# A decoder step's head: adaLN shift and scale in two halves of the features, a written order on every engine, and another product order for the first z pair

## The chip, the cores and the metric

The kernel runs on one core of one Trainium2 chip. The metric is the device time of one execution in microseconds (us), the median over runs.

## The reference

One layer of a hybrid decoder is computed for a prompt of 1024 tokens and for 8 samples of 8 tokens each (64 rows), in fp32, with a model width of 1024. What matters here is its beginning:

```python
mod = jax.nn.silu(c) @ w_ada + b_ada                  # c: 1 prompt row, 8 sample rows; w_ada 1024 x 3072
shift, scale, gate = jnp.split(mod, 3, axis=-1)
h = rmsnorm(x, norm_g) * (1 + scale[:, None]) + shift[:, None]
proj = h @ w_in                                        # w_in 1024 x 8224
u_pool, z_pool, z_ssm, xbc, dt_raw, g_raw = jnp.split(proj, SPLITS, axis=-1)
...                                                    # pooling branch, convolution, state-space scan
m = sigmoid(g_pool) * p + sigmoid(g_ssm) * s
x = x + gate[:, None] * (m @ w_o)                      # then a final rmsnorm
```

The outputs are y for prompt and samples and the new states of the pool, the convolution and the scan.

## The kernel before

All activations are held with the features on the 128 partitions and the 1088 tokens (1024 + 64) along the free axis, so h is eight tiles `k` = 0..7 of 128 x 1088. Every matmul operand is split into a rounded high half and the rest as a low half, and a product is three matmuls (high x high, high x low, low x high). Weights are split by `split` (L160): ScalarE copies the high half (L163) and GpSimd subtracts (L166).

**The head.** Tokens are cut into three blocks `BLK` of 256, 384 and 448 columns (2, 3 and 4 tiles of rows of x, the last one 64 rows). The steps are:

1. `x_load` (L195) of the first two row tiles on the SP queue, then `w_ada` for shift and scale: 16 loads (L226), per `k` one for shift and one for scale, 512 KB each. Weights of the first pair of outputs (`w_first`, L177) come between, then the other row tiles.
2. `x_norm(g3)` per block: ScalarE squares a row tile and sums it (L203), takes the root (L204), VectorE inverts and multiplies (L205, L206).
3. `x_turn` (L213): TensorE transposes the row tiles of one block for one `k` into PSUM.
4. The adaLN product (L247), 64 matmul steps into two PSUM banks `pm`; then both are copied (L259), transposed (L262) and brought into `md` (L264, L268): shift for tile `k` in `md[:, k]`, 1 + scale in `md[:, 8 + k]`.
5. `h_group(g3)` (L277): per `k`, scale and shift into `tf[k]`, the high half `hh_` on ScalarE (L311, or L299 for the first one), the low half `hl_` on VectorE or, for odd `k`, GpSimd (L283). For block 0 the source is `tf` itself (copied from PSUM at L236 or L238). For blocks 1 and 2 it is PSUM: even `k` on VectorE (L304), odd `k` on ScalarE (L302). The 64 sample columns of block 2 have a scale and shift of their own, two VectorE steps (L307, L309).
6. `first_unit` (L731): two output tiles of `g_ssm` over all eight `k`; per block and output tile 24 matmuls (L334 to L336), then ScalarE's sigmoid (L737) and a store.

**Behind it** stands a list of units: `late_loads` (L346), `dt_unit` (L631, three blocks, L638), `combine` (L446), then pairs of output tiles by Strassen's scheme. `combine` forms the sums S2, S3, S1 and S4 of quarters of h on VectorE (L465, L466, L467, L473), with high halves on ScalarE (L452) and low halves on VectorE or, for S4, on GpSimd (L453). A pair needs seven products, each of two half products of 12 matmuls with 272 columns (L534 to L536). Its weights are prepared by `pair_w` (L480): loads into `rawA`, sums on VectorE and one on GpSimd (L502), seven splits. The first pair is a z pair (`light[0]`), whose weight work carries a raised scheduling priority (`PRIO`); its products are taken in the order h11, S2, S3, S1, h12, h22, S4. Behind it comes `gate_unit(0)` (L818).

**What sets the order.** The instructions are put in order by the scheduler, from the program order, priorities and its own model of durations. In the head some instructions are bound behind others by `issue_after` with constants (`SQ`, `XT`, `TLAG`, `LAG`, `DIR`, `WK`, `PLO`). `in_line` (L1220) binds TensorE to program order in a later stage, the scan. PSUM has eight banks: three in `PA` and five in `PB`, the latter for transposes among others.

Of the kernel before, what the change touches and what calls it, by code (L numbers as in the profile page):

```python
# [14 lines left out]
PRI = 0  # L15
# [3 lines left out]
DIR = 1  # L19
LAG = 1  # L20

SQ = (1, 3, 5, 7, 7, 7, 7)
WK = 7

XT = {11: (0, 1), 12: (2, 3), 13: (4, 5), 15: (6, 7)}

PLO = (1, 3, 5, 7)
TLAG = 2
TCKW = dict(schedule_with_timeline_sim=True)

P = 128
# [25 lines left out]
def tile_pool_ssd_step(  # L57
# [140 lines left out]
    def x_norm(g3):  # L198
        for i in range((0, *XG)[g3], XG[g3]):
            xt, n = xr[i]  # L200
            sqj = pa.tile([P, D], F32, tag="rawA", name=nm("sqj"), bufs=3)
            with (tc.issue_after(h_ins[SQ[i - XG[0]]].ins) if g3 else ExitStack()):
                act(sqj[:n], xt[:n], AF.Square, accum_out=ss[:n, i:i + 1])  # L203
            act(rs[:n, i:i + 1], ss[:n, i:i + 1], AF.Sqrt, bias=eps[:n], scale=1.0 / D)  # L204
            V.reciprocal(rs[:n, i:i + 1], rs[:n, i:i + 1])  # L205
            V.tensor_scalar(xt[:n], xt[:n], rs[:n, i:i + 1], None, ALU.mult)  # L206

    def x_turn(g3, k):
        px = PB()
        c = 0  # L210
        for i in range((0, *XG)[g3], XG[g3]):
            xt, n = xr[i]
            nc.tensor.transpose(px[:, c:c + n], xt[:n, k * P:(k + 1) * P], ident[:n, :n])  # L213
            c += n
        return px

    for i in range(XG[0]):
        x_load(i)
    wraw = {}
    wbig = [Y4(hp, F32), Y4(hp, F32)]  # L220
    for k in range(KT):
        if k == WK:
            w_first = [wcols(C_G + D)(), prep(w_in[0, 0:512, C_G + D + P:C_G + D + 2 * P], 4)]
        for half in range(2):
            wraw[k, half] = wbig[k // 2][:, 2 * k % 4 + half, :D] if k < 4 else G((P, D))
            load(wraw[k, half], w_ada[0, k * P:(k + 1) * P, half * D:(half + 1) * D])  # L226
    x_norm(0)
    tf = [None] * KT

    def x0_turn(k, after=None):  # L230
        with (tc.issue_after(after.ins) if after is not None else ExitStack()):
            px = x_turn(0, k)
        w = BLK[0][1]
        tf[k] = tfp.tile([P, T], F32, tag="tf", name=nm("tf"), bufs=8)
        if k % 2:
            act(tf[k][:, :w], px[:, :w], AF.Copy)  # L236
        else:
            V.tensor_copy(tf[k][:, :w], px[:, :w])  # L238

    for k in range(KT):  # L240
        if all(k not in v for v in XT.values()):
            x0_turn(k)
    pm = [PB(), PB()]
    for k in range(KT):
        for half in range(2):
            for j in range(4):
                a_ins = mm(pm[half][32 * j:32 * j + 32, :256], scT[:, k, :], wraw[k, half][:, j * 256:j * 256 + 256],  # L247
                           start=(k == 0), stop=(k == KT - 1))
            for kx in XT.get(2 * k + half, ()):
                x0_turn(kx, a_ins)  # L250
    for i in range(XG[0], XG[1]):
        x_load(i)
    w_first[1] += prep(w_in[0, 512:1024, C_G + D + P:C_G + D + 2 * P], 4)
    for i in range(XG[1], XG[2]):
        x_load(i)
    md = const([P, 16, 9], "md")
    for half in range(2):
        mr = pa.tile([P, 256], F32, tag="rawA", name=nm("mr"), bufs=3)
        act(mr, pm[half][:, :256], AF.Copy)  # L259
        ps = PB()  # L260
        for i in range(2):
            nc.tensor.transpose(ps[:, i * P:(i + 1) * P], mr[:, i * P:(i + 1) * P], ident)  # L262
        m8 = slice(8 * half, 8 * half + 8)
        V.tensor_tensor(md[:, m8].rearrange("p (j i) b -> p j i b", i=2),  # L264
                        ps[:, :256].rearrange("p (i j b) -> p j i b", i=2, j=4)[:, :, :, 0:9],
# [8 lines left out]
    def hl_tile(k):  # L274
        return hb[1][:, k] if k < 4 else G((P, T), F32R)
# [1421 lines left out]
```

## Time and profile before

| what | value |
|---|---|
| median of 3 runs | 1329.92 us (1328.44 to 1330.29) |
| the profiled execution | 1329.25 us, its span 1327.5 us |
| granted TensorE clock, mean | 0.986 |
| TensorE busy | 1268.2 us, 96% |
| VectorE, ScalarE, GpSimd busy | 882.4, 697.3, 719.9 us |
| first product of the first pair of outputs | starts at 32.56 us |
| last product of the first z pair | starts at 111.69 us |

The profile gives start and duration of each instruction of one execution, what ended the idle time before it, and per stretch of time how long each engine was busy. PE is TensorE, PEld its weight loads, DVE VectorE, ACT ScalarE, POOL GpSimd, SP the engine whose queue issues most loads. In tables "L247" is a line of the kernel. Matmuls overlap, so durations of neighbouring ones are longer than the distance from start to start.

### The profile page before, as it was taken

Reading aid. Unit: us, or ns where it says so; the run is one execution under the profiler, and the core shown is the slowest. Engines: PE = TensorE matmul, PEld = TensorE weight load, DVE = VectorE, ACT = ScalarE, POOL = GpSimd, SP = SyncE. Lnnn points to the kernel's source line nnn. Section 1 sums busy time; section 2 is a strip of 40 time slices with the busy share of each in tenths; the row PEclk is TensorE's granted clock in tenths of the full one; section 3 lists DMA queues with packets and bytes.
Section 4 is the critical chain, followed back from the end, with each engine's and each line's share of the span. In section 5 each row is a group of like instructions: output and inputs, shape, how many; then the busy total and the mean of one; then the engine's idle time right before and its main releaser. Section 6 shows DMA issues by size and latency. Waiting matters only on the chain.

```text
span 1327.5 us, 26100 instructions
## 1 busy us (share of the span) xinstructions
PE 1268.2 (96%) x9575; PEld 1162.9 (88%) x9575; DVE 882.4 (66%) x1473; ACT 697.3 (53%) x1660; POOL 719.9 (54%) x589
## 2 busy tenths in 40 slices
PE   5889999999999999988999999999999999999998
PEld 2768999999999999978889989978987888998786
DVE  2794489778867856856566666378575777567433
ACT  3854436656656555635654464657887767301211
POOL 1357568868877876843444353456576656314000
PEclk9799999999999999989999999999999999999999
DMA  9338345635644564442557455999988665475621
GB/s 369 112 104 270 111 132 172 227 115 177 203 151 147 160 203 134 146 140 86 159 161 205 146 156 166 352 311 364 317 279 273 200 207 161 163 260 165 214 101 62
DMA packets 230521, 251.67 MB, mean 190 GB/s; under 512 B 31101, under 2 KB 173573, under 8 KB 230386
## 3 DMA queue, kind: packets, MB, share of 16 engines
q1 hardware_dynamic: 158260, 171.56, 40.7%
q10 hardware_dynamic: 72134, 78.45, 17.3%
q8 instruction: 76, 1.25, 0.4%
q14 instruction: 51, 0.42, 0.1%
HBM read 167.06 MB, written 83.01 MB: 188 GB/s over the span
## 4 chain that ended last, share of the span: by engine, by line
PE 75%; issue 7%; DVE 6%; DMA 6%; POOL 3%; ACT 3%; SPq 1%; ACTq 0%; DVEq 0%; POOLq 0%
PE ps L534 8%; PE ps L535 8%; PE ps L536 8%; PE mm L534 8%; PE mm L536 7%; PE mm L535 7%; PE mm L334 4%; PE mm L335 4%; PE mm L336 4%; PE ps L961 2%; PE ps L1645 2%; PE ps L1644 2%; PE ps L1643 2%; PE ps L1177 2%; PE ps L964 1%
## 5 line engine op out<-in xcount | busy, mean ns | idle before, releaser
L166 POOL TENSOR_TENSOR wlo<-rawA,whi 128x512 fp32r<-128x512 f32 x124 | 195.6, 1583 | 116.5 <-ACT whi L163 105.5
L166 POOL TENSOR_TENSOR wlo<-raw,whi 128x512 fp32r<-128x512 f32 x97 | 162.8, 1686 | 156.0 <-ACT whi L163 147.3
L334 PE MATMUL mm<-Y,whi 128*128 128x352 f32 (+3 forms) x504 | 172.8, 345 | 4.1 <-ACT Y L299 2.1
L335 PE MATMUL mm<-Y,whi 128*128 128x352 f32 (+3 forms) x504 | 167.0, 331 | 3.4 <-DVE Y L283 2.3
L336 PE MATMUL mm<-Y,wlo 128*128 128x352 f32 (+3 forms) x504 | 166.2, 330 | 0.0
L534 PE MATMUL mm<-Y,whi 128*128 128x272 f32 x496 | 146.3, 295 | 2.7 <-ACT dts L641 2.6
L536 PE MATMUL mm<-Y,wlo 128*128 128x272 f32 x496 | 143.4, 290 | 3.2 <-POOL wlo L166 3.2
L535 PE MATMUL ps<-Y,whi 128*128 128x272 f32 x496 | 144.1, 291 | 2.3 <-DVE Y L453 2.3
L534 PE MATMUL ps<-Y,whi 128*128 128x272 f32 x496 | 145.7, 294 | 0.0
L536 PE MATMUL ps<-Y,wlo 128*128 128x272 f32 x496 | 143.2, 289 | 0.0
L163 ACT ACTIVATE whi<-rawA 128x512 fp32r<-128x512 f32 x124 | 77.9, 628 | 123.9 <-PE ps L535 81.6
L535 PE MATMUL mm<-Y,whi 128*128 128x272 f32 x496 | 142.9, 288 | 0.0
L776 DVE SCALAR_TENSOR_TENSOR GA<-GA,cvT,GA 128x1112 f32<-128x1112 f32 x72 | 127.2, 1771 | 0.6 <-ACT GA L773 0.5
L163 ACT ACTIVATE whi<-raw 128x512 fp32r<-128x512 f32 x97 | 59.3, 627 | 94.0 <-DVE raw L502 42.3
L334 PEld LDWEIGHTS mm<-Y,whi 128*128 128x128 f32 x504 | 95.9, 191 | 11.7 <-issue 4.7
L335 PEld LDWEIGHTS mm<-Y,whi 128*128 128x128 f32 x504 | 96.4, 191 | 4.7 <-DVE Y L283 2.5
L534 PEld LDWEIGHTS mm<-Y,whi 128*128 128x128 f32 x496 | 93.4, 188 | 7.7 <-ACT dts L641 2.8
L536 PEld LDWEIGHTS mm<-Y,wlo 128*128 128x128 f32 x496 | 93.3, 188 | 4.5 <-POOL wlo L166 4.3
L534 PEld LDWEIGHTS ps<-Y,whi 128*128 128x128 f32 x496 | 94.0, 189 | 3.2 <-issue 2.9
L535 PEld LDWEIGHTS ps<-Y,whi 128*128 128x128 f32 x496 | 94.0, 190 | 3.1 <-DVE Y L453 2.7
L336 PEld LDWEIGHTS mm<-Y,wlo 128*128 128x128 f32 x504 | 96.1, 191 | 0.2
L536 PEld LDWEIGHTS ps<-Y,wlo 128*128 128x128 f32 x496 | 94.1, 190 | 0.0
(413 smaller groups left out, 3761.4 us busy)
## 6 DMA issues: line engine op xcount, KB each, us to landing
rawA<-in_w_in SPq DMA_DIRECT2D x46, 512.0 KB
dec<-acs_d SPq DMA_DIRECT2D x32, 512.0 KB
xbc<-GA ACTq DMA_DIRECT2D x24, 512.0 KB
xb<-xbc SPq DMA_DIRECT2D x32, 384.0 KB
rawA<-in_w_in SPq DMA_DIRECT2D x32, 256.0 KB
pw<-in_w_ssm_out ACTq DMA_DIRECT2D x32, 256.0 KB
ws<-ph ACTq DMA_DIRECT2D x32, 256.0 KB
ws<-pw SPq DMA_DIRECT2D x32, 256.0 KB
```

Of the source, the lines that this page charges most:

```text
L163: ins = act(hi[:, :, :ncols], raw[:, :, :ncols], AF.Copy)
L166: nc.gpsimd.tensor_tensor(lo[:, :, :ncols], raw[:, :, :ncols], hi[:, :, :ncols].bitcast(F32), ALU.subtract)
L334: mm(ps[:, :n], a, rh[k][:, o:o + n], start=(k == 0), stop=False)
L335: mm(ps[:, :n], a, rl[k][:, o:o + n], start=False, stop=False)
L336: mm(ps[:, :n], b, rh[k][:, o:o + n], start=False, stop=(k == nk - 1))
L534: mm(p, hi, ah, start=(k == 0), stop=False)
L535: mm(p, hi, al, start=False, stop=False)
L536: mm(p, lo, ah, start=False, stop=(k == 3))
L776: V.scalar_tensor_tensor(d[:, :n], rp[:, k:k + n], cvT[:, 24 * k + mc:24 * k + mc + 1], d[:, :n], ALU.mult, ALU.add)
L961: mm(o[hh], xd[:S, 2 * q + hh, :], dec[:S, 2 * q + hh], start=True, stop=state is None)
L1177: mm(pu, bt, xw.rearrange("p h d -> p (h d)"), start=True, stop=True)
L1643: mm(ps[:, :cw], mhk, wo[k][0][:, s], start=(k == 0), stop=False)
```

## The change

Shift and scale are computed in two halves of the features: part 0 for `k` 0..3, part 1 for `k` 4..7. Each load of `w_ada` now holds the part's 512 columns of shift and of scale. Five row tiles of x are loaded and normed ahead. `x_turn` copies every transposed tile to `tf`, on ScalarE or VectorE by turns, and `h_make` scales from there on VectorE for all tiles (for blocks 0 and 1 ScalarE makes the high half straight from `tf` with scale and shift). The first pair of outputs is taken by halves of the features: with `k` 0..3 for four and later five of six accumulators, then with `k` 4..7. The whole head is one function, `first`, and `in_line` binds each of the five engines to its written order there. `late_loads` is cut in two. For the first z pair the products run in the order h11, h12, h22, S2, S3, S1, S4, with the weights prepared in that order. The constants of the old order are gone.

```diff
+    def x_turn(g3, k):                       # transposes as before, then
+        o = BLK[g3][0]
+        if (k + g3) % 2:
+            act(tf[k][:, o:o + c], px[:, :c], AF.Copy)
+        else:
+            V.tensor_copy(tf[k][:, o:o + c], px[:, :c])
+    def ada_load(part, k):
+        w = wbig[k // 4][:, k % 4, :D] if part == 0 else G((P, D))
+        wraw[part, k] = w.rearrange("p (s c) -> p s c", s=2)
+        load(wraw[part, k], w_ada[0, k * P:(k + 1) * P, 0:2 * D].rearrange("p (s h c) -> p s h c", s=2, h=2)[:, :, part])
+    def ada_mm(part, k):
+        if k == 0:
+            pm[part] = PB()
+        for j in range(4):
+            mm(pm[part][32 * j:32 * j + 32, :256], scT[:, k, :], wraw[part, k][:, j // 2, j % 2 * 256:j % 2 * 256 + 256],
+               start=(k == 0), stop=(k == KT - 1))
+    def ada_end(part):                       # copy, two transposes, then scale and shift of four tiles
...
+    def h_make(g3, k):
...
+        if e == w:
+            act(hi, t, AF.Identity, scale=sc[:, 0:1], bias=sh[:, 0:1])
+        V.tensor_scalar(t[:, :e], t[:, :e], sc[:, 0:1], sh[:, 0:1], ALU.mult, ALU.add)
+        if e < w:
+            ts_ = t[:, e:w].rearrange("p (b i) -> p b i", i=8)
+            V.tensor_tensor(ts_, ts_, sc[:, 1:9].unsqueeze(2).to_broadcast([P, NB, 8]), ALU.mult)
+            V.tensor_tensor(ts_, ts_, sh[:, 1:9].unsqueeze(2).to_broadcast([P, NB, 8]), ALU.add)
+            act(hi, t, AF.Copy)
+        (nc.gpsimd if k % 2 else V).tensor_tensor(hl_[k][:, o:o + w], t, hi.bitcast(F32), ALU.subtract)
+    def in_line(engines, begin=False):       # each instruction behind the one traced before it on its engine
...
     def late_loads():                        # loads, then
+        yield
...                                           # the transposes
     def pair_w(c0, c1, pri, early):
                 diff(t2, t3, b11, ALU.add)
+                if early:
+                    add(b21)
+                    diff(b21, t2, b21, eng=nc.gpsimd)
+                    add(b21)
                 add(t2)
                 add(t3)
                 yield
                 diff(b12, b12, b11)
                 add(b12)
-                add(b21)
-                diff(t2, t2, b21, eng=nc.gpsimd)
-                add(t2)
+                if not early: ...
                 add(b22)
     def strassen(w, d0, d1, early=False):
+        if early:
+            def fifth(s, p):
+                out(d0, HF, s1, u3, ALU.subtract)(s, u3[:, s])
+                out(d1, HF, s1, c2)(s, p)
+                add(u2, u2)(s, p)
+            product(w[0], a_part(0, 0), lambda s, p: act(s1[:, s], p, AF.Copy))
+            product(w[1], a_part(0, 1), out(d0, 0, s1, c2))
+            product(w[2], a_part(1, 1), lambda s, p: act(u3[:, s], p, AF.Copy))
+            product(w[3], s_part(S2), add(s1, u2))
+            product(w[4], s_part(S3), add(u2, s1))
+            product(w[5], s_part(S1), fifth)
+            product(w[6], s4_part, out(d1, 0, u2, u2))
+            return
+    def first():
+        in_line(every, True)                  # all five engines
...
+        for i in range(5): x_load(i)
+        for k in range(KT):
+            ada_load(0, k)
+            if k == KT - 2: w_load(0, 0)
+        w_load(1, 0)
+        for i in range(5, 9): x_load(i)
+        for k in range(6): ada_load(1, k)
+        w_load(0, 1)
+        x_norm(0); x_norm(1); ada_mm(0, 0); ada_mm(0, 1); x_turn(0, 0); x_turn(0, 1)
+        x_norm(2); ada_mm(0, 2); x_turn(0, 2); x_turn(0, 3); x_norm(3); ada_mm(0, 3); x_norm(4); ada_mm(0, 4)
+        x_turn(1, 0); x_turn(1, 1); ada_mm(0, 5); x_turn(1, 2); x_turn(1, 3); ada_mm(0, 6)
+        x_turn(0, 4); x_turn(0, 5); w_split(0, 0); ada_mm(0, 7); ada_end(0)
+        h_make(0, 0..1); w_split(1, 0); h_make(0, 2..3); w_load(1, 1); ada_load(1, 6..7); next(late)
+        products(0, 0, range(4)); x_norm(5); h_make(1, 0..1); products(0, 1, range(4)); ada_mm(1, 0)
+        h_make(1, 2..3); x_norm(6); products(1, 0, range(4)); ada_mm(1, 1..2); x_norm(7); x_norm(8)
+        x_turn(0, 6); x_turn(0, 7); products(1, 1, range(4)); ada_mm(1, 3)
+        for k in range(4): x_turn(2, k); h_make(2, k)
+        x_turn(1, 4); x_turn(1, 5); products(2, 0, range(4)); ada_mm(1, 4..5); x_turn(1, 6); x_turn(1, 7); w_split(0, 1)
+        x_turn(2, 4); x_turn(2, 5); ada_mm(1, 6); w_split(1, 1); x_turn(2, 6); x_turn(2, 7); ada_mm(1, 7); ada_end(1)
+        next(late, None)
+        for bi in range(3):
+            for k in range(4, 8): h_make(bi, k)
+            for t in range(2):
+                products(bi, t, range(4 if bi < 2 or t == 0 else 0, 8))
+                done(bi, t)                   # sigmoid and store
+        in_line(every)
-    h_group(0)
-    x_norm(1)
-    x_norm(2)
-    units = [(lambda: w_first, first_unit), plain(late_loads), (dt_w, dt_unit), plain(combine), plain(to_conv),
+    first()
+    units = [(dt_w, dt_unit), plain(combine), plain(to_conv),
```

In this extract the calls of `first` are put several to a line, and `0..1` stands for a short loop or two calls; the order is that of the code.

307 lines of the change are left out of this document (170 added, 137 removed).

## The prediction

> **What bounds it now.** I read the page first, then the head in stretches, then its rows in order of time.
>
> ```profile
> PE 1268.2 (96%) x9575; PEld 1162.9 (88%) x9575; DVE 882.4 (66%) x1473; ACT 697.3 (53%) x1660; POOL 719.9 (54%) x589
> PE   5889999999999999988999999999999999999998
> PEclk9799999999999999989999999999999999999999
> ```
>
> TensorE is full from the fourth slice on. The room is in the first three slices (100 us), and the change touches nothing behind them. The stretches of the head show why; columns are start:end, length, busy us of PE, PEld, DVE, ACT, POOL, then granted clock, DMA share and GB/s.
>
> ```profile
> 25.30:32.50 7.20, 3.53 (x36) 1.75 (x36) 2.90 (x6) 3.84 (x9) 3.29 (x3) 1.00 1.07 380
> 32.50:40.50 8.00, 5.60 (x26) 5.40 (x27) 7.36 (x16) 6.22 (x17) 3.21 (x5) 0.57 0.86 271
> 40.50:49.20 8.70, 5.52 (x38) 4.13 (x37) 5.20 (x11) 8.64 (x17) 0.60 (x1) 0.89 0.55 130
> 49.20:54.40 5.20, 5.15 (x26) 5.09 (x25) 3.85 (x8) 5.18 (x13) 2.31 (x2) 0.53 0.20 68
> 54.40:74.20 19.80, 19.80 (x130) 16.29 (x129) 18.09 (x35) 10.75 (x20) 10.10 (x8) 1.00 0.08 29
> 74.20:101.70 27.50, 22.64 (x181) 17.84 (x180) 26.39 (x32) 14.82 (x28) 15.39 (x11) 1.00 0.46 141
> 101.70:111.90 10.20, 9.60 (x76) 9.24 (x74) 3.45 (x9) 6.52 (x13) 9.38 (x8) 1.00 1.01 328
> ```
>
> Until 32.5 the DMA is full and TensorE waits for the adaLN weights. From 32.5 to 101.7 VectorE is the fullest, and it and GpSimd hold each other up:
>
> ```profile
> 75.04 1.55 POOL L166 TENSOR_TENSOR wlo<-rawA,whi 128x512 fp32r<-128x512 f32 x1 [0.82 <-ACT whi L163]
> 75.36 1.82 DVE L473 TENSOR_TENSOR tf<-tf,tf 128x544 f32<-128x544 f32 x1
> 77.10 0.71 DVE L465 TENSOR_TENSOR tf<-tf,tf 128x544 f32<-128x544 f32 x1
> ```
>
> The operation that takes 0.71 us alone took 1.82 us, ending 0.6 us after GpSimd's did. So the SBUF work of the two is one queue, "the pair's time" below. The marks of the head:
>
> ```profile
> 14.97 0.64 PE L247 MATMUL ps<-Y,scT 128*32 128x256 f32 x8 [0.64 <-DMA Y<-in_w_ada]
> 16.24 0.64 PE L247 MATMUL ps<-Y,scT 128*32 128x256 f32 x8 [0.63 <-DMA Y<-in_w_ada]
> 28.82 0.64 PE L247 MATMUL ps<-G,scT 128*32 128x256 f32 x8 [0.69 <-DMA G<-in_w_ada]
> 31.91 0.60 ACT L299 ACTIVATE Y<-tf,md 128x256 fp32r<-128x256 f32 x1 [0.69 <-DVE md L268]
> 72.67 1.54 POOL L283 TENSOR_TENSOR G<-tf,G 128x448 fp32r<-128x448 f32 x1 [0.83 <-ACT G L311]
> 94.60 7.05 POOL L453 TENSOR_TENSOR Y<-tf,Y 128x544 fp32r<-128x544 f32 x4 [7.87 <-ACT Y L452]
> 111.69 0.29 PE L536 MATMUL ps<-Y,wlo 128*128 128x272 f32 x1
> 111.91 1.92 PE L818 MATMUL ps<-GA,scT 128*32 128x512 f32 x16
> ```
>
> The first scaled tile of h starts at 31.9, the last low half of h ends at 74.2, the Strassen sums end at 101.7, the first z pair at 111.9. Behind that point the program is the same, so the forecast is where 111.9 goes.
>
> **The load.** A 512 KB piece takes 16.24 - 14.97 = 1.27 us. Ahead of the last piece that the first shift and scale need stood 2 x tiles, 15 pieces and up to three quarter-megabyte weight loads; now stand 5 x tiles, 7 pieces and one. That is 5 to 6 pieces, 6.4 to 7.6 us, earlier; rows of half the length cost between nothing and a seventh of 8 x 1.27 us (380 against 328 GB/s in the rows of 25.3 and 101.7, both at a full DMA share; the latter mixes many short rows). I take 0.5, near the lower end because half a row is still longer than most of those, so 6.5. The three further norms and the turns stand in front in written order; I give them 0.5. First scaled tile: 31.9 - 6 = 26.
>
> **First half of the features, written order.** What each tile costs (mean ns is the figure behind the bar):
>
> ```profile
> L203 ACT ACTIVATE sqj<-Y 128x1024 f32<-128x1024 f32 x6 | 6.2, 1041 | 0.0
> L213 PE MATMUL ps<-ident,Y 128*128 128x128 f32 x52 | 10.0, 316 | 3.2 <-ACT tf L302 1.8 <-DVE Y L206 0.9 <-DVE tf L304 0.3
> L304 DVE TENSOR_SCALAR tf<-ps,md 128x384 f32<-128x384 f32 x8 | 5.2, 674 | 2.1 <-PE ps L213 2.1
> 37.19 0.41 DVE L304 TENSOR_SCALAR tf<-tf,md 128x256 f32<-128x256 f32 x1
> L307 DVE TENSOR_TENSOR tf<-ps,md 128x64 f32<-128x64 f32 x8 | 1.6, 217 | 0.0
> L311 ACT ACTIVATE G<-tf 128x448 fp32r<-128x448 f32 x4 | 2.3, 571 | 3.1 <-DVE tf L309 3.1
> L283 DVE TENSOR_TENSOR Y<-tf,Y 128x448 fp32r<-128x448 f32 x2 | 1.2, 622 | 0.2 <-ACT Y L311 0.2
> L283 POOL TENSOR_TENSOR Y<-tf,Y 128x256 fp32r<-128x256 f32 x2 | 1.6, 810 | 1.3 <-ACT Y L311 1.3
> L283 POOL TENSOR_TENSOR G<-tf,G 128x448 fp32r<-128x448 f32 x2 | 2.8, 1380 | 2.9 <-ACT G L311 2.9
> L166 POOL TENSOR_TENSOR wlo<-raw,whi 128x512 fp32r<-128x512 f32 x9 | 12.3, 1373 | 35.3 <-ACT whi L163 35.3
> ```
>
> Before, blocks 1 and 2 were scaled straight out of PSUM (odd tiles at L302 on ScalarE, even ones at L304 on VectorE), which took nothing from GpSimd. Now they are copied out first and scaled from SBUF on VectorE: 16 scalings of 0.41 (the 256 form) to 0.67 us join the pair's time, some 8 us. A copy of 448 columns the trace does not show: between 0.4 and 0.7 us; I take 0.7, the nearest form from PSUM. Per stage:
> - Block 0, four tiles: pair's time 4 x 0.41 + 2 x 0.42 + 2 x 0.81 + one split 1.37 = 5.5, to 31.5.
> - A norm and block 1: 0.8 + 4 x 0.5 + 2 x 0.55 + 2 x 1.1 = 6.1 with waits for ScalarE under it, less overlap 1: to 36.6.
> - Three norms (ScalarE 3 x 1.04 and their roots) beside two groups of 12 products and the next loads' products: 5, to 41.6.
> - Block 2: an even tile is copy 0.7, scale 0.5, two sample steps 0.4, high half 0.57 on ScalarE, low half 0.62, one behind the other because VectorE stands in written order: 2.8. An odd one is 0.9 plus its wait for GpSimd's 1.4 of the tile before, less overlap: 1.7. Four tiles: 9, to 50.6.
> - The tail on TensorE: four adaLN steps of 0.64, 2.6, and 22 transposes, which at 10.0 / 52 us each are 4.2 if nothing lies beside them; they alternate with those steps and with the copies, and two accumulators of the products hold two of the five banks that they turn through, so I take half, 2.1: 4.7. Then the 3.1 us from the last adaLN product to the first scaled tile (28.82 to 31.91). Second half begins at 58. The second half's loads hide under this: 13 pieces more behind the first half's 22 us, 16.5, end at 39. The last weight load among them waits on SP for a buffer that the first split frees by 25, and SP comes to it at 35; only two pieces are queued behind it.
>
> **Second half.** Twelve tiles' pair time: 4.1 + 5.5 + 7.6 = 17.2 by the same rows. Two barriers are new: in written order ScalarE passes both sigmoids of a block before the next block's high halves, and the sigmoids wait for both groups of products. Behind that wait ScalarE holds the high halves of four tiles, VectorE and GpSimd their low halves, and TensorE the next block.
>
> ```profile
> 48.73 0.47 PE L213 MATMUL ps<-ident,Y 128*128 128x128 f32 x1 [1.82 <-ACT tf L302]
> 51.36 0.41 PE L336 MATMUL mm<-G,wlo 128*128 128x256 f32 x1
> 51.58 0.41 PE L334 MATMUL mm<-G,whi 128*128 128x256 f32 x1
> L737 ACT ACT_TABLE_LOAD x2 | 2.6, 1283 | 0.0
> ```
>
> At the low clock after such a wait a 256-column product goes every 0.21 us, so 12 of them 2.6, with table load and sigmoid 4.3; block 1 at 0.17 to 0.32 us each 2 to 3.8, with its sigmoid about 3.5. VectorE runs one tile ahead under each, so I count 5.5 of 7.8. The first z pair's weights (eight GpSimd operations of 1.37 and three on VectorE, 13 us of the pair's time) go into these gaps, except 3.3 us, I judge. h ends at 58 + 17.2 + 5.5 + 3.3 = 84, against 74.2.
>
> **After h.** In the new order three products stand ahead of the first that needs a sum, so TensorE no longer waits for the sums:
>
> ```profile
> 77.96 0.36 PE L335 MATMUL mm<-G,whi 128*128 128x448 f32 x1
> 78.16 0.36 PE L336 MATMUL mm<-G,wlo 128*128 128x448 f32 x1
> 86.00 1.69 PE L638 MATMUL mm<-Y,dtw 128*32 128x448 f32 x16
> 87.50 1.69 PE L638 MATMUL mm<-G,dtw 128*32 128x448 f32 x16
> L453 DVE TENSOR_TENSOR R<-tf,R 128x544 fp32r<-128x544 f32 x3 | 2.1, 712 | 0.0
> ```
>
> 24 products of 448 columns at 0.2 (77.96 to 78.16) are 4.8, dt's last block twice the 1.5 from 86.00 to 87.50, 3, the pair's 168 products at 9.60 / 76 us (the stretch from 101.7) 21: 29, and 2 for what is late, 31. The pair's own results go out by as many VectorE operations as before and one ScalarE copy more per half, each under a half product of 12 x 0.126 = 1.5 us; the buffer that is now used twice is stored four products, 12 us, before its second use, so I cost both at nothing; were that store late, its second use would wait with one of the last two products. Sums: 28 x 0.64 to 0.71 and four on GpSimd (7.05 in the trace) are 25 to 27 us, ready at 111; the last product begins at 112, so they hide, barely. Before, it was 111.9 - 74.2 = 37.7: the order gives back 6.7 of the ten lost. The pair ends at 84 + 31 = 115, 3.1 later. The profiled run took 1329.25 (span 1327.5), so 1332.3; the median of the runs is 0.67 above it: **1333**.
>
> **Rivals.** (A) Faster: the tail runs at full clock (-2.5), weights all hide (-3.3), barriers cost 2 rather than 5.5; h ends at 74.7, the pair at 105.7, 6 earlier: 1324. For it: the start really is 6 us earlier, and the old head leaves TensorE short of work until 54.4. Against: 8 us more of the pair's time. (B) Much slower: the pair's weights, which carry a raised priority, are put between the tiles of h, so all 13 us count and not 3.3, about 10 more: 1343. It decides when a z split stands between two low halves on GpSimd; before, they ran behind the last low half, the first at 75.04. (C) No change: bursts run at full clock, so the barriers shrink by some 3 us: h at 81, pair at 112: 1330. The row at 48.73 with half-rate products behind it speaks against it, the clock of 1.00 from 25.3 to 32.5, TensorE half idle, for it. [...] (D) The order does not do what it says because the scheduler sets later work (dt, the pair's first product) into the gaps of the chain; that is B's sign with less, 1337, and I leave it inside the forecast's own range, 1330 to 1339.
>
> **How the numbers follow.** Forecast with D 0.38, A 0.30, B 0.20, C 0.12. A measurement here tells 0.2%, 2.7 us, from no change. Faster: A, and 0.04 of C. Same: 0.07 of C, 0.06 of the forecast. Slower: the rest. Range 1321 to 1344: A and B with 3 and 1 us beyond.
>
> **What would show it.** First scaled tile at 26 and the second half's at 58; ScalarE waiting for the second group's products before each sigmoid; last low half at 84; no wait of TensorE for a sum in the z pair; its end at 115. If the second half starts before 54, or h ends before 76, I am wrong on the side of A.

## The result, and the profile after

The changed kernel took 1348.93 us (median of 4 runs, 1346.56 to 1351.11) against 1329.18 for the kernel before on the same chip (4 runs): ratio 1.0155, 95% interval 1.0138 to 1.0172, some 20 us slower. Forecast were 1333 and a range up to 1344: the sign was right, the size six times too small. The profiled execution took 1346.56, its span 1344.8.

The page of the changed kernel: busy time of TensorE, then its slices of 33.6 us and the granted clock.

```profile
PE 1276.5 (95%) x9575; PEld 1167.2 (87%) x9575; DVE 888.1 (66%) x1492; ACT 699.1 (52%) x1660; POOL 716.9 (53%) x589
...
PE   4869999999999999997999999989999999999998
...
PEclk9869999999999999998999999989999999999999
```

TensorE is busy 8 us longer for the same 9575 matmuls, at a mean granted clock of 0.978 instead of 0.986, and the room is still in the first slices: the second and third now show 8 and 6 tenths, at clocks of 8 and 6 tenths. The head in stretches, cut at its own marks (start:end, length, busy us of PE, PEld, DVE, ACT, POOL, granted clock, DMA share, GB/s):

```profile
26.60:37.00 10.40, 7.61 (x34) 5.68 (x35) 9.27 (x17) 10.27 (x21) 4.87 (x5) 0.67 1.06 355
37.00:44.00 7.00, 7.00 (x58) 5.27 (x57) 2.78 (x7) 0.42 (x2) 0.04 (x1) 1.00 0.95 272
44.00:53.80 9.80, 5.85 (x26) 4.29 (x25) 6.86 (x17) 3.55 (x7) 2.42 (x2) 0.83 0.01 3
53.80:62.50 8.70, 7.46 (x63) 4.23 (x61) 2.32 (x7) 3.00 (x6) 2.55 (x2) 0.99 0.00 0
62.50:73.00 10.50, 8.50 (x37) 7.36 (x37) 4.87 (x12) 4.64 (x8) 2.74 (x3) 0.67 0.25 77
73.00:83.40 10.40, 7.67 (x24) 6.32 (x24) 5.00 (x9) 3.48 (x6) 2.34 (x2) 0.67 0.09 32
83.40:98.00 14.60, 4.61 (x11) 2.49 (x11) 12.89 (x26) 6.68 (x11) 7.10 (x2) 0.66 0.04 15
98.00:105.00 7.00, 7.00 (x26) 6.22 (x26) 7.00 (x7) 3.99 (x7) 4.71 (x3) 0.73 0.09 34
105.00:112.60 7.60, 7.60 (x98) 3.04 (x97) 6.32 (x8) 3.17 (x7) 2.04 (x2) 1.00 0.14 50
112.60:132.30 19.70, 19.70 (x162) 19.55 (x158) 8.20 (x16) 11.88 (x23) 12.54 (x10) 1.00 0.93 308
```

The marks, engines mixed in order of time:

```profile
26.59 1.09 ACT L262 ACTIVATE Y<-tf,md 128x256 fp32r<-128x256 f32 x2 [1.26 <-DVE md L239]
...
62.52 1.09 ACT L262 ACTIVATE G<-tf,md 128x256 fp32r<-128x256 f32 x2 [1.10 <-DVE md L239]
62.66 0.23 PE L319 MATMUL ps<-ident,dx 16*128 16x16 f32 x1 [0.64 <-DVE dx L316]
64.13 0.57 PE L747 MATMUL mm<-G,whi 128*128 128x256 f32 x1 [0.57 <-DVE G L269]
64.50 0.42 PE L748 MATMUL mm<-G,wlo 128*128 128x256 f32 x1
...
65.22 1.33 POOL L156 TENSOR_TENSOR wlo<-rawA,whi 128x512 fp32r<-128x512 f32 x1
...
70.71 0.38 ACT L755 ACTIVATE g<-mm 128x256 f32<-128x256 f32 x1 [4.29 <-PE mm L748]
71.07 0.28 PE L746 MATMUL mm<-G,whi 128*128 128x256 f32 x1
72.33 0.38 ACT L755 ACTIVATE g<-mm 128x256 f32<-128x256 f32 x1 [1.23 <-PE mm L748]
...
73.89 0.48 DVE L263 TENSOR_SCALAR tf<-tf,md 128x384 f32<-128x384 f32 x1 [4.92 <-ACT G L262]
...
79.75 0.49 ACT L755 ACTIVATE g<-mm 128x384 f32<-128x384 f32 x1 [4.10 <-PE mm L748]
82.59 0.49 ACT L755 ACTIVATE g<-ps 128x384 f32<-128x384 f32 x1 [2.35 <-PE ps L748]
...
84.09 0.63 DVE L269 TENSOR_TENSOR G<-tf,G 128x448 fp32r<-128x448 f32 x1 [5.10 <-ACT G L268]
...
87.11 2.99 POOL L269 TENSOR_TENSOR G<-tf,G 128x448 fp32r<-128x448 f32 x1 [8.46 <-ACT G L268]
...
93.69 0.71 DVE L431 TENSOR_TENSOR tf<-tf 128x544 f32<-128x544 f32 x1
93.82 4.11 POOL L269 TENSOR_TENSOR G<-tf,G 128x448 fp32r<-128x448 f32 x1 [3.71 <-ACT G L268]
...
96.23 0.71 DVE L432 TENSOR_TENSOR tf<-tf,tf 128x544 f32<-128x544 f32 x1
97.98 0.74 PE L747 MATMUL ps<-G,whi 128*128 128x448 f32 x1 [3.45 <-POOL G L269]
...
112.58 0.40 PE L504 MATMUL mm<-Y,whi 128*128 128x272 f32 x1
...
132.29 1.06 PE L922 MATMUL ps<-GA,scT 128*32 128x512 f32 x8
```

First tile at 26.6 (forecast 26), second half from 62.5 (forecast 58), last low half of h at 93.82 + 4.11 = 97.9 (forecast 84), z pair from 112.58 to 132.3 (forecast end 115; before 111.9). Three things are seen in the second half:

- ScalarE waits 4.29, 1.23, 4.10 and 2.35 us ahead of the four sigmoids of blocks 0 and 1, 12.0 in sum. Behind them VectorE waits 4.92 us until 73.89 and 5.10 until 84.09 for ScalarE's first high half of the next block, and is busy for 9.9 of the 20.9 us of these two blocks: the blocks stand one behind the other.
- From 62.5 to 98 TensorE has two thirds of its clock and is busy 20.8 of 35.5 us.
- In block 2 VectorE is full (12.9 of 14.6 us), but with sums of the z pair (128x544, L431, L418, L432) ahead of h's last tiles. Beside them a low half of 448 columns takes 4.11 us on GpSimd, and TensorE waits 3.45 for it.

### The profile page after: what moved, and what is told of

Its sections match the earlier page's. It is cut to its first block, busy times and chain, and to the rows that moved or that the text cites. A ratio compares the mean times of both kernels' runs of the same rounds, so it can differ in the third digit from the quotient of the medians.

```text
span 1344.8 us, 26105 instructions
## 1 busy us (share of the span) xinstructions
PE 1276.5 (95%) x9575; PEld 1167.2 (87%) x9575; DVE 888.1 (66%) x1492; ACT 699.1 (52%) x1660; POOL 716.9 (53%) x589
## 4 chain that ended last, share of the span: by engine, by line
PE 36%; issue 6%; DMA 5%; DVE 3%; ACT 3%; POOL 3%; SPq 0%; ACTq 0%; DVEq 0%; POOLq 0%
PE mm L294 4%; PE mm L296 3%; PE mm L295 3%; PE ps L1065 2%; PE ps L1734 2%; PE ps L1733 2%; PE ps L1732 2%; PE ps L1281 2%; PE ps L504 2%; PE ps L1068 2%; PE ps L505 2%; PE ps L506 2%; PE mm L504 1%; PE mm L506 1%; POOL G L1641 1%
## 5 line engine op out<-in xcount | busy, mean ns | idle before, releaser
L156 POOL TENSOR_TENSOR wlo<-rawA,whi 128x512 fp32r<-128x512 f32 x125 | 195.5, 1570 | 111.8 <-ACT whi L153 105.9
L156 POOL TENSOR_TENSOR wlo<-raw,whi 128x512 fp32r<-128x512 f32 x96 | 159.8, 1673 | 152.8 <-ACT whi L153 144.0
L294 PE MATMUL mm<-Y,whi 128*128 128x352 f32 (+1 forms) x480 | 163.5, 341 | 0.9 <-DVE G L1635 0.5
L295 PE MATMUL mm<-Y,whi 128*128 128x352 f32 (+1 forms) x480 | 157.2, 328 | 1.0 <-DVE Y L1316 1.0
L296 PE MATMUL mm<-Y,wlo 128*128 128x352 f32 (+1 forms) x480 | 156.8, 327 | 0.0
L153 ACT ACTIVATE whi<-raw 128x512 fp32r<-128x512 f32 x96 | 58.6, 628 | 95.0 <-DVE raw L467 37.7
L504 PEld LDWEIGHTS mm<-Y,whi 128*128 128x128 f32 x496 | 93.3, 188 | 4.9 <-ACT u L608 1.7
L506 PEld LDWEIGHTS mm<-Y,wlo 128*128 128x128 f32 x496 | 93.3, 188 | 4.4 <-POOL wlo L156 4.1
L294 PEld LDWEIGHTS mm<-Y,whi 128*128 128x128 f32 x480 | 90.3, 188 | 7.4 <-issue 4.3
L506 PEld LDWEIGHTS ps<-Y,wlo 128*128 128x128 f32 x496 | 94.8, 191 | 0.6 <-POOL wlo L156 0.6
L505 PEld LDWEIGHTS ps<-Y,whi 128*128 128x128 f32 x496 | 94.8, 191 | 0.3 <-issue 0.2
L505 PEld LDWEIGHTS mm<-Y,whi 128*128 128x128 f32 x496 | 93.4, 188 | 0.1
L295 PEld LDWEIGHTS mm<-Y,whi 128*128 128x128 f32 x480 | 90.4, 188 | 1.7 <-DVE Y L1316 1.6
```

What stands on the lines that cost most here:

```text
L153: ins = act(hi[:, :, :ncols], raw[:, :, :ncols], AF.Copy)
L156: nc.gpsimd.tensor_tensor(lo[:, :, :ncols], raw[:, :, :ncols], hi[:, :, :ncols].bitcast(F32), ALU.subtract)
L294: mm(ps[:, :n], a, rh[k][:, o:o + n], start=(k == 0), stop=False)
L295: mm(ps[:, :n], a, rl[k][:, o:o + n], start=False, stop=False)
L296: mm(ps[:, :n], b, rh[k][:, o:o + n], start=False, stop=(k == nk - 1))
L504: mm(p, hi, ah, start=(k == 0), stop=False)
```

## The experiments

The experiments were run in four series, each with its own runs of the kernel before (medians 1326.3 to 1327.4), so kernels of different series are compared by their ratio; 0.1% is 1.3 us.

| kernel | median us | ratio to before (95%) | first tile | second half | last low half | z pair ends |
|---|---|---|---|---|---|---|
| before (profile) | 1329.9 | 1 | 31.9 | | 74.2 | 111.9 |
| changed | 1348.9 | 1.0155 (1.0138, 1.0172) | 26.6 | 62.5 | 97.9 | 132.3 |
| a_free | 1322.7 | 0.9968 (0.9952, 0.9985) | 25.2 | 51.4 | 73.1 | 107.8 |
| a_done | 1341.8 | 1.0116 (1.0091, 1.0140) | 29.3 | 65.3 | 91.7 | 127.1 |
| a_comb | 1345.2 | 1.0142 (1.0118, 1.0166) | 27.9 | 64.2 | 91.7 | 129.3 |
| b_early | 1326.2 | 0.9988 (0.9977, 1.0000) | 33.3 | | 75.7 | 111.8 |
| a_act | 1337.2 | 1.0079 (1.0054, 1.0105) | 23.9 | 56.1 | 82.6 | 116.8 |
| a_nact | 1341.2 | 1.0110 (1.0093, 1.0127) | 25.1 | 64.0 | 90.8 | 126.2 |
| a_pe | 1336.4 | 1.0063 (1.0038, 1.0088) | 26.3 | 60.5 | 78.4 | 121.6 |
| a_all3 | 1335.3 | 1.0062 (1.0046, 1.0077) | 29.6 | 66.8 | 85.1 | 121.4 |
| a_free_old | 1320.5 | 0.9952 (0.9939, 0.9966) | 25.0 | 51.3 | 73.0 | 108.9 |
| a_noearly | 1349.2 | 1.0167 (1.0151, 1.0183) | 30.6 | 66.7 | 102.4 | 137.2 |
| a_free_sums | 1318.4 | 0.9936 (0.9923, 0.9948) | 25.2 | 50.4 | 68.5 | 103.6 |
| a_free_both | 1319.4 | 0.9943 (0.9929, 0.9957) | 24.9 | 51.0 | 69.1 | 104.2 |
| a_head | 1347.5 | 1.0155 (1.0136, 1.0175) | 26.4 | 56.3 | 94.8 | 129.0 |
| a_all4 | 1331.5 | 1.0038 (1.0024, 1.0053) | 27.6 | 56.7 | 76.4 | 113.2 |
| a_all3_p | 1331.3 | 1.0040 (1.0024, 1.0056) | 24.3 | 57.1 | 77.6 | 114.0 |
| a_sums_old | 1319.6 | 0.9952 (0.9940, 0.9964) | 26.2 | 52.1 | 70.1 | 105.5 |

The marks come from one execution of each kernel, in us. With the same loads in front of it the first tile begins at different times (why is told below, under "The first tile"), so stretches are counted from it.

### a_free: the change without the written order

```diff
-        in_line(every, True)
...
-        in_line(every)
```

> The changed kernel without the written order in the head: the halves of the features, the two steps of the sample part, the copies out of PSUM and the new order of the z pair's products stay, and the scheduler orders the engines. Theory O (the written order itself, its two waits of ScalarE for a block's products above all, costs most of the 19.8 us): the last low half of h comes 8 to 12 us earlier than 97.9, and the time is 1334 to 1341. Rival H (the work by halves has too much in it: 16 more scalings on VectorE, copies that wait for PSUM, the sums drawn between the tiles): the last low half stays at 94 or later and the time is 1345 or more. If the scheduler does better than before with the halves, the time is under 1330; nothing in the profile of the changed kernel speaks for that.

Measured: 1322.7 us, ratio 0.9968, 0.3% faster than before. All of the loss belongs to the written order, (1.0155 - 0.9968) of 1327 = 25 us, more than theory O said, and the halves with the new order of the products are a gain of 0.3%, for which nothing in the changed kernel's profile had spoken. Rows of a_free in order of time:

```profile
25.15 1.08 ACT L262 ACTIVATE Y<-tf,md 128x256 fp32r<-128x256 f32 x2
...
51.40 1.19 ACT L262 ACTIVATE G<-tf,md 128x256 fp32r<-128x256 f32 x2
...
66.74 5.33 POOL L269 TENSOR_TENSOR G<-tf,G 128x256 fp32r<-128x256 f32 x1 [4.21 <-DVE tf L263]
66.97 0.71 DVE L431 TENSOR_TENSOR tf<-tf 128x544 f32<-128x544 f32 x1
...
107.78 1.06 PE L920 MATMUL ps<-GA,scT 128*32 128x512 f32 x8
```

From the first tile to the second half 51.40 - 25.15 = 26.3 us, against 62.52 - 26.59 = 35.9 with the written order; from there to the last low half 21.6 against 35.4. A low half of only 256 columns takes 5.33 us on GpSimd beside the sums on VectorE: that fault is the scheduler's too.

### a_done: the sigmoids behind the next block's high halves

```diff
         for bi in range(3):
             for k in range(4, 8):
                 h_make(bi, k)
+            if bi:
+                for t in range(2):
+                    done(bi - 1, t)
             for t in range(2):
                 products(bi, t, range(4 if bi < 2 or t == 0 else 0, 8))
-                done(bi, t)
+        for t in range(2):
+            done(2, t)
```

> The two sigmoids of a block are written behind the next block's high halves, all else as in the changed kernel. Theory O (barriers): ScalarE's waits of 4.29, 1.23, 4.10 and 2.35 us ahead of the sigmoids hold the next block's tiles; they add up to 12.0, of which VectorE ran one tile ahead under each, so 6 to 9 us come back: 1340 to 1343, and TensorE runs the second half at a higher granted clock than 0.67. Rival H: the tiles wait for VectorE and GpSimd, which are short in any case, and the gap is filled again: 1346 to 1349, with the last low half still at 95 or later.

```profile
73.62 0.39 ACT L755 ACTIVATE g<-mm 128x256 f32<-128x256 f32 x1 [2.01 <-PE mm L748]
75.16 0.39 ACT L755 ACTIVATE g<-mm 128x256 f32<-128x256 f32 x1 [1.15 <-PE mm L748]
...
87.61 4.11 POOL L269 TENSOR_TENSOR G<-tf,G 128x448 fp32r<-128x448 f32 x1 [3.71 <-ACT G L268]
```

The stretch from the first tile to the last low half falls from 71.3 to 62.4 us, the time to 1341.8, as theory O had it (by the ratios the gain is 0.0039 of 1327, 5.2 us). The two waits of block 0 are 3.2 us instead of 5.5, and of those of block 1 (6.5) 0.4 is left. The granted clock from 62 to 100 us is 0.73 (0.72 up to 74, 0.74 behind) instead of 0.66, higher as theory O said. The low half beside the sums is untouched: 4.11 us again.

### a_comb: the z pair's sums behind the last step of h on VectorE

```diff
+    def combine_behind():
+        with behind(mybir.EngineType.DVE):
+            combine()
...
-        (nc.gpsimd if k % 2 else V).tensor_tensor(hl_[k][:, o:o + w], t, hi.bitcast(F32), ALU.subtract)
+        (nc.gpsimd if k % 2 and (g3, k) != (2, 7) else V).tensor_tensor(hl_[k][:, o:o + w], t, hi.bitcast(F32), ALU.subtract)
...
-    units = [(dt_w, dt_unit), plain(combine), plain(to_conv),
+    units = [(dt_w, dt_unit), plain(combine_behind), plain(to_conv),
```

> The sums of the z pair are bound behind the last step of h on VectorE, and the low half of the last tile runs on VectorE instead of GpSimd; all else as in the changed kernel. Theory S (sums drawn ahead of the last tiles): low halves of 2.99 and 4.11 us on GpSimd beside sums on VectorE, against 1.1 to 1.3 us alone, and 6 sums of about 0.7 us ahead of the last tiles put off the end of h: it ends at 88 to 91 rather than 97.9, and the time is 1340 to 1342 provided that the sums, begun later by as much, still are ready for the fourth product of the pair. Rival: the end of h comes earlier, but the sums come later by as much and TensorE waits for them in the z pair, so that 0 to 3 us are left: 1346 to 1349.

```profile
88.03 1.14 POOL L269 TENSOR_TENSOR G<-tf,G 128x448 fp32r<-128x448 f32 x1 [7.58 <-ACT G L268]
...
91.07 0.62 DVE L269 TENSOR_TENSOR G<-tf,G 128x448 fp32r<-128x448 f32 x1 [0.64 <-ACT G L268]
...
105.33 0.96 PE L630 MATMUL mm<-Y,dtw 128*32 128x448 f32 x8 [2.48 <-ACT g L759]
...
129.28 1.07 PE L926 MATMUL ps<-GA,scT 128*32 128x512 f32 x8
```

The low half on GpSimd, 2.99 us at this tile in the changed kernel, takes 1.14, and the last one ends at 91.7, inside the stretch 7.5 us less (63.8): the mechanism holds. The time, 1345.2, lies between the two expectations, and by the ratios the gain (1.7 us) can't be told from none. From the last low half to the end of the pair it is now 37.6 us, not 34.4: TensorE waited 2.48 for an accumulator that a sigmoid had to free. A first tile 1.3 us later took another part.

### b_early: the kernel before with the new order of the z pair alone

```diff
-        return pair(c0, c0 + P, to_dram(func, d[0]), to_dram(func, d[1]), PRIO if c0 == C_Z else PRI)
+        return pair(c0, c0 + P, to_dram(func, d[0]), to_dram(func, d[1]), PRIO if c0 == C_Z else PRI, c0 == C_Z)
```

> The kernel before with one part of the change alone: the z pair's products and weight sums in the new order (three products that need no sum first). The prediction's step says that the order alone gives back 6.7 us of the 37.7 from the last low half to the end of the pair: 1323 to 1325. Rival: what TensorE waited for there was only a part of that, 27.50 - 22.64 = 4.9 us without matmul from 74.2 to 101.7, and the scheduler had filled what could be filled: 1326 to 1329. If the weights that are needed earlier in the new order come late, or the buffer that is used twice is not free, it is slower than 1330.

```profile
74.12 1.54 POOL L283 TENSOR_TENSOR G<-tf,G 128x448 fp32r<-128x448 f32 x1 [0.83 <-ACT G L311]
...
111.83 1.06 PE L845 MATMUL ps<-GA,scT 128*32 128x512 f32 x8
```

From the last low half (75.66) to the end of the pair it is 36.2 us, against 37.7 before. The order alone is worth 1.6 us with an interval from 0 to 3.1: the rival's size, not the 6.7 of the prediction.

### a_act, a_nact, a_pe: the written order on some engines only

```diff
-        every = (ET.PE, ET.Activation, ET.DVE, ET.Pool, ET.SP)
+        every = (ET.Activation,)                    # a_act
+        every = (ET.PE, ET.DVE, ET.Pool, ET.SP)     # a_nact
+        every = (ET.PE,)                            # a_pe
```

> The changed kernel with the written order on ScalarE alone; the other engines are ordered by the scheduler. Without any written order the time was 1322.7, with it on all five 1348.9. Theory A (ScalarE's order, with its two waits for a block's products, is the main cost): two thirds of those 26 us or more remain, 1338 or more. Rival E (no engine's order costs much by itself, the orders have to hold each other): 1323 to 1331.

> The written order on TensorE, VectorE, GpSimd and the load queue, with ScalarE left to the scheduler. Theory A: the sigmoids go behind the high halves, and 8 to 13 us come back at the least (8.9 us earlier was the end of h when the sigmoids alone were moved): 1336 to 1341 or less. Rival V (VectorE's written order, in which the copies and scalings of one tile wait for PSUM and hold those of the next, is the larger part): 1341 or more.

> The written order on TensorE alone. The second half's turns then still stand where they are written, ahead of the last adaLN products, and its start at about 62 is kept, but ScalarE, VectorE and GpSimd are free. Theory A: most comes back, 1322 to 1330. Rival T (TensorE's written order, which lets it run no later work while it waits for a tile, is the larger part): 1335 or more.

Above a_free's ratio these are 0.0111, 0.0142 and 0.0095, that is 15, 19 and 13 us of the 25. a_pe came out as rival T had it. a_act (1337.2) lies between its expectations, just under theory A's 1338, and a_nact (1341.2) at the border of its two. No engine's order is the cause by itself: with ScalarE free three quarters of the loss stay (a_nact), which speaks against theory A, and with ScalarE's order alone more than half of it is there (a_act), against rival E. The costs don't add up, 15 + 19 is more than the whole. That fits one engine in a poor order holding the others: in a_act ScalarE waits 5.51 and 6.36 us ahead of the sigmoids of two blocks, in a_pe TensorE waits 6.86 for one low half. TensorE's order alone puts the second half off to 34.2 us behind the first tile (26.3 without).

### a_all3: three mendings, all in written order

a_done and a_comb together, and the z pair's weights at normal priority:

```diff
-        return pair(c0, c0 + P, to_dram(func, d[0]), to_dram(func, d[1]), PRIO if c0 == C_Z else PRI, c0 == C_Z)
+        return pair(c0, c0 + P, to_dram(func, d[0]), to_dram(func, d[1]), PRI, c0 == C_Z)
```

> All in written order, with the sigmoids behind the next block's high halves, the z pair's sums bound behind the last step of h on VectorE with the last low half there too, and the z pair's weights at normal priority. The first two took 8.9 and 7.5 us off the stretch from the first high half to the last low half (71.3 us), but only 7.1 and 3.7 off the time. If they add up and the weights (three steps on VectorE, 2.1 us, and one split) also go: stretch 52 to 56, time 1333 to 1338. If one wait takes the place of another: 1338 to 1342.

Measured 1335.3, and a stretch of 85.1 - 29.6 = 55.5 us: as expected, the mendings add up in the stretch. The second half takes 18.3 us instead of 35.4 (66.79 to 85.10). By the ratios they bring 12.3 of the 25 us.

### a_head, a_all4, a_all3_p: what the other half is

a_head writes the end of the first half in another order, with block 2's first products and the weight splits behind the moved steps; a_all4 is the same with the three mendings; a_all3_p has the mendings and leaves TensorE to the scheduler.

```diff
         ada_mm(1, 3)
-        for k in range(4):
-            x_turn(2, k)
-            h_make(2, k)
+        x_turn(2, 0)
+        x_turn(2, 1)
+        ada_mm(1, 4)
+        h_make(2, 0)
...
         x_turn(1, 6)
         x_turn(1, 7)
-        w_split(0, 1)
+        ada_mm(1, 7)
+        h_make(2, 3)
...
-        ada_mm(1, 7)
+        w_split(1, 1)
         ada_end(1)
+        products(2, 0, range(4))
```

> The changed kernel, all in written order, with only the end of its first half written in another order: the turns of the second half's features and the last four adaLN steps stand between the four tiles of block 2 instead of behind them. In the changed kernel the second half's first tile began 35.9 us behind the first tile of all (62.52 - 26.59), without written order 26.3 us (51.40 - 25.15). Theory W (what stands where in the written order, not the order as such): the second half begins 27 to 31 us behind the first tile and the time falls by 4 to 8, to 1341 to 1345. Rival: copies out of PSUM and scalings are then in each other's way on VectorE, the begin stays at 34 or more and the time at 1347 or more.

> The same, with the three mendings of before (sigmoids behind the next high halves, the z pair's sums behind h, its weights at normal priority), all in written order: it was 1335.3 without the moved turns. Theory W: another 5 to 9 us, 1326 to 1330, near the kernel before. Rival R (TensorE's written order costs by itself, since nothing later may run in its waits): 1332 or more.

> The three mendings with the turns where they were written, and TensorE alone left to the scheduler. Theory W: the scheduler draws the adaLN steps and the turns forward on TensorE, but their copies stay where they are written on VectorE and ScalarE, so the begin of the second half moves by less than half of the ten us: 1330 to 1334. Rival R: 1322 to 1328.

a_head:

```profile
56.34 0.60 ACT L262 ACTIVATE G<-tf,md 128x256 fp32r<-128x256 f32 x1 [1.68 <-DVE md L239]
...
68.18 0.39 ACT L755 ACTIVATE g<-mm 128x256 f32<-128x256 f32 x1 [5.22 <-PE mm L748]
...
90.69 4.11 POOL L269 TENSOR_TENSOR G<-tf,G 128x448 fp32r<-128x448 f32 x1 [3.72 <-ACT G L268]
```

The second half begins 29.9 us behind the first tile, as theory W said, 6 earlier than in the changed kernel. The last low half is only 3.1 us earlier: the waits ahead of the sigmoids (5.22, 1.02, 4.10, 1.96) are still 12.3 in sum, and the low half beside the sums again takes 4.11. The 4 to 8 us of time that theory W forecast did not come: the median (1347.5) and the ratio (1.0155, as in the changed kernel) show no gain, and by the time alone the rival is right, though its reason, a start at 34 or more, is not. Only the profiled execution was 3.7 us shorter (span 1341.1).

a_all4:

```profile
27.64 1.09 ACT L262 ACTIVATE Y<-tf,md 128x256 fp32r<-128x256 f32 x2 [1.25 <-DVE md L239]
...
56.66 0.60 ACT L262 ACTIVATE G<-tf,md 128x256 fp32r<-128x256 f32 x1 [1.70 <-DVE md L239]
...
75.80 0.62 DVE L269 TENSOR_TENSOR G<-tf,G 128x448 fp32r<-128x448 f32 x1 [0.64 <-ACT G L268]
...
113.24 1.06 PE L935 MATMUL ps<-GA,scT 128*32 128x512 f32 x8
```

With the mendings the same move takes the ratio from 1.0062 to 1.0038, 3.2 us, with intervals that just overlap. The time falls between W and R. The stretch to the last low half is 48.8 us (a_free: 47.9), so h is mended. What is left, 0.0070 or 9 us by the ratios, is 5.5 us in the profiles (end of the z pair 113.24 against 107.78): 2.5 at the first tile, 0.9 in h, 2.1 behind it. a_all3_p, 1.0062 to 1.0040 with intervals overlapping, came out as theory W had it, in the time and in the second half, which begins 32.8 us behind the first tile instead of 37.2. How the last 9 us divide was not settled.

### a_free_old, a_noearly, a_sums_old: what the new order of the z pair is worth

```diff
-PRIO if c0 == C_Z else PRI, c0 == C_Z)
+PRIO if c0 == C_Z else PRI)
```

> The halves of the features and the new load order alone: no written order, and the z pair's products in their old order. With the new order of the products it was 1322.7 against 1327.4 before. Theory: the order of the products is worth the 1 to 2 us that it brought in the kernel before (1326.2 against 1327.4; from the last low half to the end of the pair 36.2 rather than 37.7 us), so 1323 to 1325. Rival: the order is what makes the halves pay, because the scheduler has the sums ready later here, and without it the time is 1327 or more.

> The changed kernel with the z pair's products and weight sums in the old order. Theory: in the changed kernel the sums were ready 1.3 us before the pair began, so the order of the products is worth 0 to 2 us here: 1348 to 1351. The prediction's step (the order gives back 6.7 us) would make it 1354 to 1357.

> No written order, the z pair's sums bound behind h, and the z pair's products in the old order (with the new order: 1318.35). Here the sums come later, so the order that needs none for three products should count: 1320 to 1323. Rival: dt's products and the sigmoids' groups already cover the sums, and the order is worth nothing: 1317.5 to 1319.5.

Without written order the old order gives 0.9952 and the new one 0.9968; in the changed kernel 1.0167 and 1.0155; with the sums bound behind h 0.9952 and 0.9936. All three pairs of intervals overlap, and the signs differ. In these kernels the order can't be told from nothing: a_noearly came out as expected, a_free_old was faster than either of its expectations, a_sums_old lies at their border.

### a_free_sums, a_free_both: a version that beats both

a_free with the edit of a_comb, and (a_free_both) the weights at normal priority as well.

> No written order, and the z pair's sums bound behind the last step of h that stands on VectorE in the program, with the last tile's low half on VectorE. Without the binding a pair of low halves took 6.31 us on GpSimd beside sums on VectorE, and TensorE waited 3.23 and 2.43 us for low halves. Theory S: these waits go, the last low half comes 3 to 4 us earlier than 73.05, and the time is 1318 to 1321. Rival: the sums then come later by as much and the pair waits for them: 1322 to 1325.

> As the last, and the z pair's weights at normal priority. Three differences of weights stood on VectorE at 55.8 to 61.5 among the tiles, 0.68, 1.65 and 1.48 us. If they cost what they hold, another 2 to 3 us: 1316 to 1319. Rival: they come too late for the second and third product of the pair, which wait for them: 1321 or more.

Rows of a_free_sums:

```profile
63.53 3.97 POOL L269 TENSOR_TENSOR G<-tf,G 128x256 fp32r<-128x256 f32 x1 [3.54 <-DVE tf L263]
...
67.55 0.39 PE L750 MATMUL mm<-G,whi 128*128 128x256 f32 x1 [1.57 <-POOL G L269]
```

1318.4 us, ratio 0.9936 (0.9923 to 0.9948), as theory S had it: the fastest kernel here, 8.5 us under the one before. The last low half ends at 68.5, 43.3 us behind the first tile (47.9 without the binding). TensorE's wait there is 1.57 instead of 2.43 us, and the other one 0.84 instead of 3.23. The weights' priority makes no difference that shows: a_free_both, 1319.4 us and 0.9943, lies between its two expectations.

## Why the prediction was right or wrong, point by point

The pair ended 17.3 us later than forecast (132.3 for 115): 4.5 of them arose in the first half, 9.4 in the second and 3.4 behind it.

**What bounds it: read too broadly.** "From 32.5 to 101.7 VectorE is the fullest" does not hold in every stretch shown: from 40.5 to 54.4 ScalarE is fuller (8.64 and 5.18 us against 5.20 and 3.85), from 54.4 to 74.2 TensorE (19.80 of 19.80).

**The first tile: right in sum, 26 forecast and 26.6 measured, by two errors that nearly cancel.** The landing was right: by the sum the last adaLN step could start at 22.3 (28.82 - 6.5), and the last load that it needs landed at 21.8 (in a_act TensorE waits for it, until 21.86). But that step, the last of these rows, began at 24.04, because the turns of block 1 are written ahead of it and wait for norms on VectorE:

```profile
19.56 0.33 PE L205 MATMUL ps<-ident,Y 128*128 128x128 f32 x1 [1.45 <-DVE Y L194]
20.93 0.66 PE L205 MATMUL ps<-ident,Y 128*128 128x128 f32 x4 [1.04 <-DVE Y L194]
...
24.04 0.64 PE L227 MATMUL ps<-Y,scT 128*32 128x256 f32 x8
```

So the term "norms and turns in front, 0.5" was 2.2, and the way from there to the first tile 2.6 instead of 3.1. Over the experiments the first tile began between 23.9 (a_act) and 30.6. In a_noearly, the latest, the eight products of each of the two steps at 23.51 and 26.00 took 1.08 us instead of 0.64, and the last step began at 28.05.

**First half, 26 to 58: 4.5 us short.** Blocks 0 and 1 came as summed, 31.97 and 37.04 (forecast 31.5 and 36.6). The next term, 5 us for two groups of products, the loads' products and three norms, was 7.0: I summed ScalarE's norms there, and the bound was TensorE, busy 7.0 of 7.0 us at full clock. Block 2's four tiles took 9.8 instead of 9, and the tail 8.7 instead of 7.8, TensorE busy for 7.46 of it. What I did not see is that this tail need not stand where it is written: the scheduler interleaves it with block 2 and begins 10 us earlier (a_free).

**Second half, 26 us forecast, 35.4 measured.** This is the step that failed. The term "barriers, 5.5 of 7.8" was mis-sized: I took the pair's time of all twelve tiles (17.2) as the bound and added what is not covered, with VectorE one tile ahead under each barrier. In fact VectorE was busy 9.9 of 20.9 us in blocks 0 and 1; each block was a chain of tiles, products at half rate and sigmoids, 10.5 and 10.4 us long, with nothing of block 1 under the first and one scaled tile of block 2 under the second. VectorE scales a tile in place, so it waits until ScalarE has read that tile for the high half (4.92 us, until 73.89). Moving the sigmoids alone took 8.9 us off the stretch, against the 5.5. The second cause was in no term: the z pair's sums on VectorE ahead of the last tiles, and GpSimd starved beside them, 7.5 us of stretch in a_comb. I had the sums ready "at 111" and so asked only whether they come too late, not whether they come too early; yet the profile of the kernel before has such sums between its last tiles (L465 at 68.68, L466 at 69.58, the last low half ending at 74.2). The term for the tiles (17.2) held: with the sigmoids, the sums and the weights moved out of the way the second half took 18.3 us (a_all3).

**The weights: as rival B's point of decision has it, at a smaller price.** A z split does stand between two low halves (65.22 us, between those at 64.54 and 69.10), with three differences on VectorE. a_free_both shows no gain from putting them back where nothing else is in written order; in the written order they were tried only together with the other two.

**After h: 31 forecast, 34.4 measured.** The products of the last block took 7.0 instead of 4.8 (clock 0.73), dt 7.6 instead of 3, the pair 19.7 instead of 21 (one of its fourteen half products had run before), and no wait for a sum was seen, as said. The step that failed is dt: I counted its last block alone, as in the kernel before, but none of its three blocks had found room ahead. And so "the order gives back 6.7" is wrong: b_early has 1.6.

**The rivals.** A (1324) is near what the halves give without the written order, for another reason than its terms: not a faster tail and short barriers, but none. B and D named the right family, later work drawn between the tiles of h, but not the piece that cost: B the weights, D dt and the pair's first product, rather than the sums. Half of that product did run inside block 0 (twelve matmuls of 272 columns from 64.93 on), without cost: the last tile's low half ended at 69.82, and its product began at 69.88. C fell: the granted clock in the second half is 0.66 to 0.67. Ahead of the half rate at 64.50 (0.42 us for 256 columns, 0.28 at 71.07) TensorE's longest wait since the clock had returned at 53.9 was 0.64, at 62.66. It was busy for only 0.64 us between 62 and 64, and the clock fell at 64.2.

## What to carry to other kernels

Before an order is written out by hand on several engines, follow each engine's queue through it: an instruction that waits for the end of a group holds all that is written behind it, and the price is the whole chain of the group, not the part of it that exceeds the fullest engine. Binding a single piece of work can pay where binding all does not: here one binding (the sums behind h, with one low half moved to VectorE) on top of the scheduler's order took the ratio from 0.9968 to 0.9936, where the full order raised it to 1.0155. And ask of work that is "hidden" not only whether it comes late, but whether it may be drawn forward between the operations that others wait for.

## What the runs showed of the hardware that was not expected

- A subtraction on GpSimd of 128x448 takes 1.14 us beside an idle VectorE (52.63 in the changed kernel) and 2.99 or 4.11 beside a run of two-input operations on VectorE, which keep 0.71 us each (93.69 to 96.23); one of 128x256 took 5.33 (66.74 in a_free) instead of 0.73. The prediction had seen the two hold each other up by 1.1 us in one operation (1.82 for 0.71); beside the 4.11 no operation of VectorE was longer, and GpSimd's ended only behind VectorE's run, at 97.93, 0.99 behind the last operation of the run (96.23 + 0.71). VectorE's copies of 448 columns out of PSUM did not show this: 0.62 us at 57.83 and 59.76, each beside a split on GpSimd (1.27 and 1.28), and 0.62 at 43.88 with GpSimd idle.
- After the clock had fallen to a half at 64.2 us, it took until 71.0 to return, though TensorE was busy for 6.6 of these 6.8 us; it fell again at 74.4 and 88.1 and returned at 81.2 and 101.7, the last time when the products from 98 on had run for 3.7. In the profiles of the kernel before and of the changed one the clock fell eight times and returned eight times between 19 and 140 us, and within each profile two such changes in a row are 3.4, 6.8, 10.2 or 13.7 us apart. In the 3.4 us ahead of the eight falls TensorE was busy for 0.55 to 1.94 us, in the 3.4 us ahead of the eight returns for 3.00 to 3.41. These figures give no sharp limit: after 3.4 us with 1.57 (from 91.64 in the kernel before) the clock stayed full, after 3.4 us with 3.14 (from 64.17 in the changed kernel) it stayed at a half.
- The last load that the first tile needs landed at 21.8 in the changed kernel and at 21.86 in a_act, but the first tile behind it began at 26.6 and 23.9, and over the profiles up to 6.7 us apart (23.9 to 30.6): TensorE waits for norms (1.45 and 1.04 us in the rows under "The first tile"), and in a_noearly two steps took 1.08 us instead of 0.64. How much each of the two took in each profile was not separated.
